# Forgetting sums: a product on TensorE, or loaded across the partitions and added by VectorE

## The chip, the cores and the metric

The kernel runs on one core of a Trainium2 chip. The metric is the device time of one execution in microseconds; lower is better. TensorE multiplies matrices into PSUM, VectorE, ScalarE and GpSimd work element by element, and SyncE issues every DMA of this kernel, in one queue.

## The reference

One decoder block over 512 tokens and 16 meta tokens ahead of them (L = 528). All is f32. One projection of the normed input feeds two attentions of 16 heads each, whose outputs are gated, mixed and normed. The forgetting attention (FoX) adds a sum of log forget gates to its scores:

```python
log_f = jax.nn.log_sigmoid((f_logit + fox_forget_b[l]).astype(jnp.float32)).transpose(0, 2, 1)
cum = jnp.cumsum(log_f, axis=-1)
...
s = jnp.einsum('bhqd,bhkd->bhqk', qb, k, preferred_element_type=jnp.float32) * scale
if cq is not None:
    s = s + (cq[..., :, None] - cum[:, :, None, :])
s = jnp.where(key_pos[None, :] <= qpos[:, None], s, -jnp.inf)
p = jax.nn.softmax(s, axis=-1)
```

The term of the query (`cq`) is the same for a whole row and falls out of the softmax, so only `-cum` of the keys has to reach the scores: one number for each key and head, the same for every query.

## The kernel before

TensorE's instructions stand in the order of the program text; the other engines' are ordered by a scheduler with priorities, and some DMAs are kept in the order of the text. After an opening (norm, small projections, the forget sums) come sixteen attention stages, a forgetting stage and a latent (MLA) stage in turn, each for two heads: `stages = [(br, pr) for pr in range(8) for br in (1, 0)]`, `br` 1 is forgetting. Then the gates and output products follow.

A stage computes scores of all 512 queries of two heads in four query blocks `b` of 128. Block `b` sees 144 + 128 b keys, and only its last 128 need the causal mask. `scores(0)` does blocks 0 to 2 in two PSUM banks a head (0 and 1 together, then 2), `scores(1)` does block 3 in two pieces. Every f32 operand is split into a high and a low half, so a product of two is three products (`hlk`, `hlq` are the split keys and queries). The two heads lie on partitions 0 to 63 and 64 to 127, so a product is a pair of 64-row matmuls, one for each head.

In a forgetting stage there is a fourth pair: the sums `CT` (two rows a head, high and low half of `-cum / SC_FOX`) times `ONE`, which is one on these two rows and zero elsewhere. It spreads the sums over the 128 queries inside the accumulation. `CT` is loaded for each head pair from `c_dram` by two small DMAs, issued from `k_fox`.

Behind the products VectorE reads each piece of scores out of PSUM with one instruction that adds the mask `maskt`, scales by `-scale`, writes `sf` and keeps the smallest value `nb`; a second piece of a block takes the first one's `nb` along. ScalarE takes the exponential in place and sums it up (`su`). `norm` (`n0`, `n1`) scales by `ri`, the reciprocal of `su`, and writes high and low f16 halves `pn` (ScalarE the high, VectorE the low, GpSimd those of the meta keys). DMA transposes bring `pn` into `ptt`, and `values`, which runs in the next stage between its two score parts, multiplies by the values into `ov`; VectorE turns that into `gT`.

Between these parts TensorE works on `fill`: the projections of the gates `z`, and of the next stage's queries, keys and values (`fq`, `fk`, `v`, `mq`, `mk`). They accumulate in three PSUM banks (`accp`), which each take the next result when the one in them has been read: `mq` is read by ScalarE and VectorE into `hlq`, `mk` into `hlk`, `z` into `sil`. Weights come in as `wraw` by DMA and are split into `wh` (ScalarE) and `wl` (GpSimd).

In a forgetting stage the fill is: the gate `z` of the forgetting branch, `mq`, three eighths of the latent branch's `z`, `mk` in two halves, then the rest of that `z` with `v` between.

Of the kernel before, what the change touches and what calls it, by code (L numbers as in the profile page):

```python
# [11 lines left out]
F32 = mybir.dt.float32  # L12
# [5 lines left out]
ALU = mybir.AluOpType  # L18
# [5 lines left out]
S = 512  # L24
META = 16
L = S + META
NH = 16
KD = D // 128
# [10 lines left out]
SC_FOX = 1.0 / math.sqrt(HD)  # L39
NEG = -1.0e30  # L40
# [5 lines left out]
HALF = 272  # L46
# [3 lines left out]
def f32(ap):  # L50
    return ap.bitcast(F32)
# [3 lines left out]
def block_kernel(ctx: ExitStack, tc: tile.TileContext, x, meta_tokens, pre_norm_g, w_in, fox_forget_b,  # L55
                 mla_q_norm_g, mla_kv_norm_g, w_uq, w_ukv, w_br_mla, w_br_fox, w_out, post_norm_g,
                 rope_tok, rope_pe, out):
    nc = tc.nc
# [18 lines left out]
    padp = ctx.enter_context(tc.tile_pool(name="padp", bufs=1, side="right"))  # L77
    pad = padp.tile([128, 56], F32, tag="pad", name="pad")

    c_dram = dram.tile([2, NH, L], F32, tag="cdram", name="c_dram")  # L80
    qpe_dram = dram.tile([NH, 2, 2, 16, S], F32, tag="qpedram", name="qpe_dram")

    wp = ctx.enter_context(tc.tile_pool(name="wp", bufs=3))
    uid = [0]
    written, sums_out = [False], []
    behind, through, first_t, exps, halved, lowered = [], [], [], [], {}, {}

    def dma(out, src, start=None):

        with tc.issue_after(sums_out[1]) if written[0] and len(sums_out) == 2 else nullcontext():  # L90
            ins = (start or nc.sync.dma_start)(out=out, in_=src)
        if written[0]:
            tc.keep_in_program_order(ins)
        return ins.ins

    def mm(*a, **k):
        nc.tensor.matmul(*a, **k)  # L97
# [75 lines left out]
    ths = {}  # L173
# [66 lines left out]
    def hl_done(key, n, w):  # L240

        def done(i, ps):
            if i == 0:
                hls[key] = hlp.tile([128, 2, n], F32R, tag=f"hl{key[0]}", name="hl" + "".join(map(str, key)))
            hl = hls[key]
            o = w * i
            w_ = min(w, n - o)

            with tc.high_priority(offset=30):
                halved[key, i] = nc.scalar.copy(hl[:, 0, o : o + w_], ps).ins  # L250
                lowered[key, i] = split_lo(nc.vector, hl[:, 1, o : o + w_], ps, hl[:, 0, o : o + w_]).ins
        return done
# [2 lines left out]
        return unit(f"fq{pr}", win_w(O_FQ, pr), u_act, KD, REAL, hl_done(("q", 1, pr), S, S))  # L255

    def k_fox(pr):
        halves = hl_done(("k", 1, pr), L, HALF)

        def done(i, ps):  # L260
            halves(i, ps)
            if pr and i:
                for h in range(2):

                    with tc.issue_after(first_t[0]) if pr == 1 else nullcontext():
                        dma(f32(CT[64 * h : 64 * h + 2, :]), c_dram[:, 2 * pr + h, :])
        return unit(f"fk{pr}", win_w(O_FK, pr), u_act, KD, ALLT, done)

# [3 lines left out]
    with ExitStack() as ph:  # L272
# [265 lines left out]
        for i in range(2):  # L538
            for h in range(2):
                nc.sync.dma_start(f32(CT[64 * h + i : 64 * h + i + 1, :]), f32(ch[h : h + 1, i]))  # L540
        for i in range(2):
            sums_out.append(nc.sync.dma_start(c_dram[i], f32(ch[:, i])).ins)

    gctx = ctx.enter_context(ExitStack())
    PAIRED = [i + 4 * j for i in range(4) for j in range(2)]
# [2 lines left out]
    def gate_unit():  # L548

        i, br = gates.pop(0)  # L550

        def done(_, ps):
            ths[i, br] = thp.tile([128, S], F32, tag="th", name=f"th{i}{br}")
            nc.scalar.activation(ths[i, br], ps, AF.Tanh, scale=0.5)
        return unit(f"pg{i}{br}", win_w((O_GA, O_GB)[br], i), u_act, KD, REAL, done)


    with ExitStack() as att:
# [4 lines left out]
        stp = att.enter_context(tc.tile_pool(name="stp", bufs=4, space=PSUM))  # L563
        ovp = att.enter_context(tc.tile_pool(name="ovp", bufs=1, space=PSUM))

        QP = ac.tile([128, S], F32R, tag="QP", name="QP")
        maskt = ac.tile([128, L + 16], BF16, tag="maskt", name="maskt")
        nc.gpsimd.memset(maskt, 0.0)
# [177 lines left out]
        def attention(br, pr):  # L746
# [6 lines left out]
            def sets(h, b, c0, w):  # L753
                hs = slice(64 * h, 64 * h + 64)
                qs, ks = slice(128 * b, 128 * b + 128), slice(c0, c0 + w)
                out = [(q[hs, i, qs], k[hs, j, ks]) for i, j in ((0, 0), (1, 0), (0, 1))]
                if br:
                    return out + [(ONE[hs], CT[hs, ks])]
                return out + [(QP[hs, qs], KP[i][hs, ks]) for i in range(2)]

            sums, sfs = {}, {}
# [2 lines left out]
            def sf_of(h, b):  # L764
                o, n = SF_STEP * (b % 3), 144 + 128 * b
                return sfs[b // 3][:, h, o : o + n]

            def scores(g):

                banks = (((0, 0, 144, 0), (1, 0, 272, 144)), ((2, 0, 400, 0),)) if g == 0 else \  # L770
                    (((3, 0, HALF, 0),), ((3, HALF, L - HALF, 0),))

                def fn():
                    if g == 0:
                        for t in ("nb", "su", "ri"):
                            sums[t] = aw.tile([128, 2, 4], F32, tag=t, name=f"{t}{nm_}")
                    sfs[g] = aw.tile([128, 2, (2 * SF_STEP + 400, L)[g]], F32, tag=f"sf{g}", name=f"sf{nm_}{g}", bufs=1)
                    for ib, parts in enumerate(banks):
                        ps = [stp.tile([128, 512], F32, tag="st", name=f"st{nm_}{g}{ib}{h}") for h in range(2)]
                        for b, c0, w, o in parts:  # L780
                            for i, ops in enumerate(zip(*(sets(h, b, c0, w) for h in range(2)))):
                                for h, (Q, K) in enumerate(ops):
                                    mm(ps[h][:, o : o + w], Q, K, start=(i == 0), stop=(i == 4 - br))
                        for b, c0, w, o in parts:
                            m0 = 384 - 128 * b + c0
                            for h in range(2):
                                nb = sums["nb"][:, h, b : b + 1]

                                with tc.high_priority(offset=100):
                                    nc.vector.tensor_tensor_reduce(  # L790
                                        out=sf_of(h, b)[:, c0 : c0 + w], in0=ps[h][:, o : o + w],
                                        in1=maskt[:, m0 : m0 + w], scale=-scale, scalar=3.0e38 if c0 == 0 else nb,
                                        op0=ALU.add, op1=ALU.min, accum_out=nb)
                    with tc.high_priority(offset=60):
                        for b in GRP[g]:
                            for h in range(2):
                                sf = sf_of(h, b)
                                exps[g] = nc.scalar.activation(sf, sf, AF.Exp, bias=sums["nb"][:, h, b : b + 1],  # L798
                                                               scale=-1.0, accum_out=sums["su"][:, h, b : b + 1]).ins
                return fn  # L800
# [45 lines left out]
                                               op0=ALU.mult, op1=ALU.mult)  # L846

            return scores(0), scores(1), norm(0), norm(1), values

        def in_order():  # L850

# [57 lines left out]
        behind.clear()  # L909
        late = []  # L910
        for si, (br, pr) in enumerate(stages):
            s0, s1, n0, n1, va = attention(br, pr)

            fill = fills[si]
            for fn in [s0] + late:
                fn()
            if si == 0:
                run(fill[:3])
            s1()

            if si == 0:

                run(fill[3:5])
                run(vts[1, 0] + pe_rest)
# [6 lines left out]
                first_t.extend(through)  # L931
                run(fill[5:])
            else:
                if si == 1:

                    written[0] = True
                    for x in range(2):
                        store0(x, 2, 8)
                    written[0] = False
                run(fill[:5])  # L940
                if si == 1:

                    behind[:] = exps[:1]
# [254 lines left out]
```

## Time and profile before

| | us |
|---|---|
| median of three runs | 600.92 (600.5 to 601.12) |
| the profiled execution | 601.22 |
| its span in the profile | 599.2 |
| TensorE busy | 590.7 |
| VectorE, ScalarE, GpSimd busy | 374.3, 342.4, 179.4 |

Some 2 us lie around the span. Rows of the profile read: start or busy time, engine, line of the kernel, operation, the tile written and those read, and the shape. The granted TensorE clock is 0.999 of full speed. The kernel moved 58.10 MB from HBM and 4.00 MB to it.

### The profile page before, as it was taken

The page shows a single profiled execution, that of the slowest core. Times are in us where ns is not written, and L with a number is a line of the kernel's source. Part 1 is how long each engine was busy: PE and PEld are TensorE (multiplying, and loading weights), DVE is VectorE, ACT ScalarE, POOL GpSimd, SP SyncE. Part 2 cuts the span into 40 slices and gives each one's busy share as a digit, 9 for nine tenths or more (in the row PEclk, how much of TensorE's full clock was granted, in tenths as well). Part 3 has the DMA queues.
Part 4 walks back from the last instruction along what each step waited for, and adds up shares of the span by engine and source line. Part 5 has one row for each costly group of instructions (what it writes and reads, how often), then busy time and mean ns, then how long its engine had stood idle before and what let it go on. Part 6 is the DMA issues. An engine that isn't in the chain of part 4 may idle for free.

```text
span 599.2 us, 10724 instructions
## 1 busy us (share of the span) xinstructions
PE 590.7 (99%) x3777; PEld 501.3 (84%) x3777; DVE 374.3 (62%) x1004; ACT 342.4 (57%) x786; POOL 179.4 (30%) x239
## 2 busy tenths in 40 slices
PE   8999999999999999999999999999999999999996
PEld 6989889889889888898898898878888888888884
DVE  5946776774675675766657747764633524367857
ACT  7847775784674675766758747852222423353753
POOL 4316544444348353433524534430000000000000
PEclk9999999999999999999999999999999999999999
DMA  8532889988885998796896878788534333333603
GB/s 288 117 83 88 158 177 250 205 184 181 159 163 124 200 212 203 143 200 139 172 192 136 179 157 176 170 161 291 175 85 106 106 92 84 105 106 93 224 0 141
DMA packets 217910, 93.22 MB, mean 156 GB/s; under 512 B 131372, under 2 KB 209588, under 8 KB 217856
## 3 DMA queue, kind: packets, MB, share of 16 engines
q1 hardware_dynamic: 217856, 92.54, 66.3%
q8 instruction: 29, 0.48, 0.3%
q14 instruction: 25, 0.20, 0.1%
HBM read 58.10 MB, written 4.00 MB: 104 GB/s over the span
## 4 chain that ended last, share of the span: by engine, by line
PE 96%; ACT 2%; DMA 1%; issue 0%; SPq 0%; DVE 0%; POOL 0%; DVEq 0%; ACTq 0%; POOLq 0%
PE z L97 17%; PE pg L97 15%; PE py L97 15%; PE st L97 9%; PE v L97 9%; PE fk L97 8%; PE fq L97 8%; PE ov L97 5%; PE x L97 4%; PE psm L97 3%; PE mq L97 2%; PE mk L97 1%; PE ppe L97 1%; PE y L97 1%; DMA wsr<-in_w_in_dram 1%; ACT uTh L382 0%
## 5 line engine op out<-in xcount | busy, mean ns | idle before, releaser
L103 POOL TENSOR_TENSOR wl<-wraw,wh 128x1024 fp32r<-128x1024 f32 (+2 forms) x62 | 120.1, 1945 | 104.2 <-ACT wh L130 75.6
L130 ACT CAST wh<-wraw 128x1024 fp32r<-128x1024 f32 (+1 forms) x80 | 83.0, 1041 | 115.7 <-PE pg L97 38.5
L798 ACT ACTIVATE sf<-sf,nb 128x144 f32<-128x144 f32 (+3 forms) x128 | 72.0, 564 | 8.3 <-DVE nb L790 8.2
L826 DVE SCALAR_TENSOR_TENSOR pn<-sf,ri,pn 128x128 f16<-128x128 f32 (+3 forms) x128 | 68.7, 575 | 12.4 <-ACT pn L825 12.3
L825 ACT ACTIVATE pn<-sf,ri 128x128 f16<-128x128 f32 (+3 forms) x128 | 61.5, 551 | 19.9 <-ACT sf L798 17.2
L103 DVE TENSOR_TENSOR wl<-wraw,wh 128x1024 fp32r<-128x1024 f32 x34 | 41.6, 1223 | 43.7 <-ACT wh L130 43.5
L790 DVE CUSTOM_DVE_ANT_0 sf<-st,maskt 128x272 f32<-128x272 f32 (+2 forms) x128 | 48.7, 435 | 4.0 <-PE st L97 3.9
L97 PE MATMUL z<-uTh,wh 128*128 128x512 f32 x128 | 50.9, 398 | 0.0
L97 PE MATMUL pg<-uTh,wh 128*128 128x512 f32 x128 | 50.3, 393 | 0.0
L97 PE MATMUL z<-uTl,wh 128*128 128x512 f32 x128 | 50.0, 391 | 0.0
L97 PE MATMUL z<-uTh,wl 128*128 128x512 f32 x128 | 50.0, 390 | 0.0
L97 PE MATMUL pg<-uTl,wh 128*128 128x512 f32 x128 | 49.8, 389 | 0.0
L97 PE MATMUL pg<-uTh,wl 128*128 128x512 f32 x128 | 49.8, 389 | 0.0
L97 PE MATMUL py<-gh,wh 128*128 128x512 f32 x128 | 49.8, 389 | 0.0
L97 PE MATMUL py<-gl,wh 128*128 128x512 f32 x128 | 49.8, 389 | 0.0
L97 PE MATMUL py<-gh,wl 128*128 128x512 f32 x128 | 49.8, 389 | 0.0
L97 PE MATMUL st<-hlk,hlq 64*128 64x272 f32 (+3 forms) x480 | 47.3, 306 | 0.0
L97 PEld LDWEIGHTS st<-hlk,hlq 64*128 64x128 f32 x480 | 35.0, 185 | 5.8 <-ACT vh L722 2.8
L703 DVE TENSOR_REDUCE vsc<-v 128x1 f32<-128x272 f32 (+1 forms) x32 | 13.2, 432 | 37.9 <-PE v L97 37.9
L97 PE MATMUL v<-uTh,wl 128*128 128x256 f32 (+1 forms) x128 | 36.5, 285 | 0.0
L97 PE MATMUL fk<-uTl,wh 128*128 128x256 f32 (+1 forms) x128 | 36.4, 285 | 0.0
L97 PE MATMUL fk<-uTh,wh 128*128 128x256 f32 (+1 forms) x128 | 36.4, 285 | 0.0
(233 smaller groups left out, 1430.1 us busy)
## 6 DMA issues: line engine op xcount, KB each, us to landing
wraw<-in_w_in_dram SPq DMA_DIRECT2D x56, 512.0 KB
wraw<-in_w_br_fox_dram SPq DMA_DIRECT2D x8, 512.0 KB
tb<-in_w_out_dram SPq DMA_DIRECT2D x8, 512.0 KB
wraw<-in_w_br_mla_dram SPq DMA_DIRECT2D x8, 512.0 KB
wraw<-in_w_out_dram SPq DMA_DIRECT2D x6, 512.0 KB
xr<-in_x_dram SPq DMA_DIRECT2D x4, 512.0 KB
out_dram<-yo SPq DMA_DIRECT2D x8, 256.0 KB
QP<-qpe_dram SPq DMA_DIRECT2D x7, 256.0 KB
```

Of the source, the lines that this page charges most:

```text
L97: nc.tensor.matmul(*a, **k)
L103: return eng.tensor_tensor(out=lo, in0=src, in1=f32(hi), op=ALU.subtract)
L130: nc.scalar.copy(wh[:, :n], raw[:, :n])
L703: nc.vector.tensor_reduce(out=sc[:, i : i + 1], in_=ps, op=ALU.max, axis=AX.X, apply_absolute_value=True)
L790: nc.vector.tensor_tensor_reduce(out=sf_of(h, b)[:, c0 : c0 + w], in0=ps[h][:, o : o + w], in1=maskt[:, m0 : m0 + w], scale=-scale, scalar ...
L798: exps[g] = nc.scalar.activation(sf, sf, AF.Exp, bias=sums["nb"][:, h, b : b + 1], scale=-1.0, accum_out=sums["su"][:, h, b : b + 1]).ins
L825: nc.scalar.activation(hi, sf, AF.Copy, scale=rib)
L826: nc.vector.scalar_tensor_tensor(out=lo, in0=sf, scalar=rib, in1=hi, op0=ALU.mult, op1=ALU.subtract)
```

## The change

In the seven forgetting stages of head pairs 1 to 7 the fourth pair of products is gone. The sums of both heads are loaded from `c_dram` once a pair, each spread over 128 partitions by the load itself (`cbp`). GpSimd makes a second copy with the causal mask in it (`cbm`: the meta columns copied, the 512 others through a select). VectorE's reduce adds these f32 tiles in place of the bf16 mask. Since a block's unmasked and masked columns now stand in two tiles, a reduce over both becomes two (`added`). `c_dram` holds one f32 row a head instead of two halves, made by one GpSimd multiply. The two pairs of tiles live in the pool of the gates' results `th`, whose tiles grow from 512 to 528 columns. Pair 0 keeps its product.

```diff
-    c_dram = dram.tile([2, NH, L], F32, tag="cdram", name="c_dram")
+    c_dram = dram.tile([NH, L], F32, tag="cdram", name="c_dram")
...
     def k_fox(pr):
-        halves = hl_done(("k", 1, pr), L, HALF)
-
-        def done(i, ps):
-            halves(i, ps)
-            if pr and i:
-                for h in range(2):
-
-                    with tc.issue_after(first_t[0]) if pr == 1 else nullcontext():
-                        dma(f32(CT[64 * h : 64 * h + 2, :]), c_dram[:, 2 * pr + h, :])
-        return unit(f"fk{pr}", win_w(O_FK, pr), u_act, KD, ALLT, done)
+        return unit(f"fk{pr}", win_w(O_FK, pr), u_act, KD, ALLT, hl_done(("k", 1, pr), L, HALF))
...
-        for i in range(2):
-            sums_out.append(nc.sync.dma_start(c_dram[i], f32(ch[:, i])).ins)
+        nc.gpsimd.tensor_scalar(out=fa[:, 2], in0=fa[:, 0], scalar1=-1.0 / SC_FOX, scalar2=None, op0=ALU.mult)
+        sums_out.append(nc.sync.dma_start(c_dram, fa[:, 2]).ins)
...
+        cb = [[thp.tile([128, L], F32, tag="th", name=f"cb{n}{h}") for h in range(2)] for n in "pm"]
...
                 if br:
-                    return out + [(ONE[hs], CT[hs, ks])]
+                    return out if pr else out + [(ONE[hs], CT[hs, ks])]
...
+            def added(h, b, c0, c1):
+
+                if not (br and pr):
+                    return [(c0, c1, maskt[:, 384 - 128 * b + c0 : 384 - 128 * b + c1])]
+                d = META + 128 * b if b else 0
+                return [(a, e, cb[n][h][:, a:e]) for n, a, e in ((0, c0, min(c1, d)), (1, max(c0, d), c1)) if a < e]
...
                                 nb = sums["nb"][:, h, b : b + 1]
-
-                                with tc.high_priority(offset=100):
-                                    nc.vector.tensor_tensor_reduce(
-                                        out=sf_of(h, b)[:, c0 : c0 + w], in0=ps[h][:, o : o + w],
-                                        in1=maskt[:, m0 : m0 + w], scale=-scale, scalar=3.0e38 if c0 == 0 else nb,
-                                        op0=ALU.add, op1=ALU.min, accum_out=nb)
+                                for a, e, in1 in added(h, b, c0, c0 + w):
+
+                                    with tc.high_priority(offset=100):
+                                        nc.vector.tensor_tensor_reduce(
+                                            out=sf_of(h, b)[:, a:e], in0=ps[h][:, o + a - c0 : o + e - c0],
+                                            in1=in1, scale=-scale, scalar=3.0e38 if a == 0 else nb,
+                                            op0=ALU.add, op1=ALU.min, accum_out=nb)
...
+        def bias(pr):
+
+            for h in range(2):
+                plain, masked = cb[0][h], cb[1][h]
+                nc.sync.dma_start(plain, c_dram[2 * pr + h : 2 * pr + h + 1].broadcast_to([128, L]))
+                nc.gpsimd.tensor_copy(masked[:, 0:META], plain[:, 0:META])
+                nc.gpsimd.affine_select(out=masked[:, META:].rearrange("p (b c) -> p b c", c=128),
+                                        in_=plain[:, META:].rearrange("p (b c) -> p b c", c=128),
+                                        pattern=[[0, 4], [-1, 128]], base=0, channel_multiplier=1,
+                                        compare_op=ALU.is_ge, fill=NEG)
...
                 n0()
+                if not (br or last):
+                    bias(pr + 1)
                 run(fill[5:11])
```

The scheduler places the other engines' instructions anew. VectorE in the forgetting stage of pair 1, from the second bank of `scores(0)` into `scores(1)`; before (`ISA` rows are the reduces, those of `nb` alone read out the minimum):

```order
L790 ISA sf_1443,nb_1440<-st_1466,maskt 128x400
L790 ISA nb_1440 128x1
L790 ISA sf_1443,nb_1440<-st_1467,maskt 128x400
L790 ISA nb_1440 128x1
L806 TENSOR_SCALAR su_1441<-su_1441 128x2x3
L807 RECIPROCAL ri_1442<-su_1441 128x2x3
L845 SCALAR_TENSOR_TENSOR gT_777<-ov_1484,vsc_1094,sil_1121 128x512
L826 SCALAR_TENSOR_TENSOR pn_724<-sf_1443,ri_1442,pn_724 128x128
L790 ISA sf_1512,nb_1440<-st_1513,maskt 128x272
L790 ISA nb_1440 128x1
L790 ISA sf_1512,nb_1440<-st_1514,maskt 128x272
L790 ISA nb_1440 128x1
```

and now:

```order
L791 ISA sf_1455,nb_1452<-st_1476,cbp_718 128x272
L791 ISA nb_1452 128x1
L791 ISA sf_1455,nb_1452<-st_1477,cbm_721,nb_1452 128x128
L791 ISA nb_1452 128x1
L791 ISA sf_1455,nb_1452<-st_1476,cbm_720,nb_1452 128x128
L791 ISA nb_1452 128x1
L846 SCALAR_TENSOR_TENSOR gT_781<-ov_1494,vsc_1098,sil_1125 128x512
L791 ISA sf_1522,nb_1452<-st_1523,cbp_718 128x272
L791 ISA nb_1452 128x1
L791 ISA sf_1522,nb_1452<-st_1524,cbp_719 128x272
L791 ISA nb_1452 128x1
L791 ISA sf_1522,nb_1452<-st_1533,cbp_718,nb_1452 128x128
```

The block of 400 columns is read in 272 and 128, with `nb` as a further operand of the second; `su`, `ri` and the first `pn` no longer stand ahead of the last block.

ScalarE in the same stage, from the exponentials (`sf`) to `hlq`; before:

```order
L798 ACTIVATE sf_1443,su_1441<-sf_1443,nb_1440 128x272
L798 ACTIVATE sf_1443,su_1441<-sf_1443,nb_1440 128x400 x2
L825 ACTIVATE pn_724<-sf_1443,ri_1442 128x128 x2
L825 ACTIVATE pn_724<-sf_1443,ri_1442 128x2x128 x2
L825 ACTIVATE pn_724<-sf_1443,ri_1442 128x3x128 x2
L798 ACTIVATE sf_1512,su_1441<-sf_1512,nb_1440 128x528 x2
L825 ACTIVATE pn_725<-sf_1512,ri_1442 128x4x128 x2
L130 CAST wh_1806<-wraw_1544 128x1024
L738 ACTIVATE sil_1593<-z_1546 128x512
L250 CAST hlq_1611<-mq_1604 128x512
```

and now:

```order
L799 ACTIVATE sf_1455,su_1453<-sf_1455,nb_1452 128x400 x2
L799 ACTIVATE sf_1522,su_1453<-sf_1522,nb_1452 128x528 x2
L826 ACTIVATE pn_728<-sf_1455,ri_1454 128x128 x2
L826 ACTIVATE pn_728<-sf_1455,ri_1454 128x2x128 x2
L826 ACTIVATE pn_728<-sf_1455,ri_1454 128x3x128 x2
L826 ACTIVATE pn_729<-sf_1522,ri_1454 128x4x128
L730 ACTIVATE sil_1601<-z_1554 128x512
L826 ACTIVATE pn_729<-sf_1522,ri_1454 128x4x128
L130 CAST wh_1814<-wraw_1552 128x1024
L250 CAST hlq_1619<-mq_1612 128x512
```

The exponentials of the last block (528 columns) come ahead of all `pn`, and `sil` moves between the last two `pn`; the weight cast still stands ahead of `hlq`.

SyncE's queue behind the same stage's scores; before:

```order
L91 DMA wraw_1619<-in_w_in_dram 128x8x128
L91 DMA CT<-c_dram 2x528
L91 DMA_TRANSPOSE pt<-pn_724 128x6x128
L91 DMA CT<-c_dram 2x528
L91 DMA_TRANSPOSE pt<-pn_724 128x10x128
L91 DMA_TRANSPOSE pt<-pn_724 128x14x128
L91 DMA_TRANSPOSE pt<-pn_725 128x18x128
L91 DMA wraw_1810<-in_w_in_dram 128x8x128
```

and now:

```order
L91 DMA wraw_1627<-in_w_in_dram 128x8x128
L855 DMA cbp_718<-c_dram 128x528
L855 DMA cbp_719<-c_dram 128x528
L91 DMA_TRANSPOSE pt<-pn_728 128x6x128
L91 DMA_TRANSPOSE pt<-pn_728 128x10x128
L91 DMA_TRANSPOSE pt<-pn_728 128x14x128
L91 DMA_TRANSPOSE pt<-pn_729 128x18x128
L91 DMA wraw_1818<-in_w_in_dram 128x8x128
```

The loads of the next pair's sums stand ahead of the stage's four transposes; the loads into `CT` that stood among them are gone.

More of the change, by code (lines that the diff above doesn't have):

```diff
@@ L85, in block_kernel @@
     written, sums_out = [False], []
-    behind, through, first_t, exps, halved, lowered = [], [], [], [], {}, {}
+    behind, through, exps, halved, lowered = [], [], [], {}, {}
     def dma(out, src, start=None):
-        with tc.issue_after(sums_out[1]) if written[0] and len(sums_out) == 2 else nullcontext():
+        with tc.issue_after(sums_out[0]) if written[0] and sums_out else nullcontext():
             ins = (start or nc.sync.dma_start)(out=out, in_=src)
@@ L552, in done @@
         def done(_, ps):
-            ths[i, br] = thp.tile([128, S], F32, tag="th", name=f"th{i}{br}")
+            ths[i, br] = thp.tile([128, L], F32, tag="th", name=f"th{i}{br}")[:, 0:S]
             nc.scalar.activation(ths[i, br], ps, AF.Tanh, scale=0.5)
@@ L766, in sf_of @@
                 return sfs[b // 3][:, h, o : o + n]
+            last_set = (4, 2 if pr else 3)[br]
+            def added(h, b, c0, c1):
[3 more added lines that the diff above has]
+                return [(a, e, cb[n][h][:, a:e]) for n, a, e in ((0, c0, min(c1, d)), (1, max(c0, d), c1)) if a < e]
             def scores(g):
@@ L782, in fn @@
                                 for h, (Q, K) in enumerate(ops):
-                                    mm(ps[h][:, o : o + w], Q, K, start=(i == 0), stop=(i == 4 - br))
+                                    mm(ps[h][:, o : o + w], Q, K, start=(i == 0), stop=(i == last_set))
                         for b, c0, w, o in parts:
-                            m0 = 384 - 128 * b + c0
                             for h in range(2):
                                 nb = sums["nb"][:, h, b : b + 1]
-                                with tc.high_priority(offset=100):
-                                    nc.vector.tensor_tensor_reduce(
-                                        out=sf_of(h, b)[:, c0 : c0 + w], in0=ps[h][:, o : o + w],
-                                        in1=maskt[:, m0 : m0 + w], scale=-scale, scalar=3.0e38 if c0 == 0 else nb,
-                                        op0=ALU.add, op1=ALU.min, accum_out=nb)
+                                for a, e, in1 in added(h, b, c0, c0 + w):
[4 more added lines that the diff above has]
+                                            op0=ALU.add, op1=ALU.min, accum_out=nb)
                     with tc.high_priority(offset=60):
@@ L911, in block_kernel @@
         for si, (br, pr) in enumerate(stages):
+            last = si + 1 == len(stages)
             s0, s1, n0, n1, va = attention(br, pr)
@@ L930, in block_kernel @@
                 n1()
-                first_t.extend(through)
                 run(fill[5:])
```

## The prediction

> **What bounds the kernel now.** I read the page first: its busy line, then the chain that ended last.
>
> ```profile
> PE 590.7 (99%) x3777; PEld 501.3 (84%) x3777; DVE 374.3 (62%) x1004; ACT 342.4 (57%) x786; POOL 179.4 (30%) x239
> PE 96%; ACT 2%; DMA 1%; issue 0%; SPq 0%; DVE 0%; POOL 0%; DVEq 0%; ACTq 0%; POOLq 0%
> ```
>
> TensorE is the bound: 96% of the chain is its own work, no other engine holds over 2%. An instruction taken off TensorE shortens the program by its issue time, unless a result of another engine then comes too late. So two things are wanted: the price of the removed products, and the waits that stand just behind TensorE. The timeline of the second forgetting stage (head pair 1, 103.27 to 122.40 us) shows both. First TensorE (start, duration, instruction; merged rows have a count).
>
> ```profile
> 103.27 0.56 PE L97 MATMUL st<-hlk,hlq 64*128 64x144 f32 x6
> 103.66 0.28 PE L97 MATMUL st<-CT,ONE 64*128 64x144 f32 x2
> 103.77 0.58 PE L97 MATMUL st<-hlk,hlq 64*128 64x272 f32 x6
> 104.19 0.28 PE L97 MATMUL st<-CT,ONE 64*128 64x272 f32 x2
> 104.32 0.72 PE L97 MATMUL st<-hlk,hlq 64*128 64x400 f32 x6
> 104.86 0.36 PE L97 MATMUL st<-CT,ONE 64*128 64x400 f32 x2
> ...
> 107.60 0.29 PE L97 MATMUL st<-CT,ONE 64*128 64x272 f32 x2
> 107.72 0.51 PE L97 MATMUL st<-hlk,hlq 64*128 64x256 f32 x6
> 108.07 0.28 PE L97 MATMUL st<-CT,ONE 64*128 64x256 f32 x2
> ...
> 117.70 0.35 PE L97 MATMUL mk<-cTh,wh 128*128 128x256 f32 x1
> 117.89 0.28 PE L97 MATMUL mk<-cTl,wh 128*128 128x256 f32 x1
> ...
> 122.40 0.56 PE L97 MATMUL st<-hlk,hlq 64*128 64x144 f32 x6
> ```
>
> The durations overlap; what counts is start to next start. A pair of products (one for each head) takes one slot: three 400-wide pairs fill 104.32 to 104.86, 0.18 us each.
>
> The two rows of `mk` show the only place in the stage where TensorE already slips. The second half of the latent keys (`mk`) takes over the accumulator bank that `mq` filled, so it must wait until VectorE has read `mq` into `hlq`. Its first product lasts 0.35 instead of 0.28 us, and the next starts 0.07 us late. VectorE's rows at this place, here and in a later forgetting stage (head pair 6), with TensorE's matching row of that one:
>
> ```profile
> 116.93 0.68 DVE L103 TENSOR_TENSOR hlq<-mq,hlq 128x512 fp32r<-128x512 f32 x1
> ...
> 330.45 0.68 DVE L103 TENSOR_TENSOR hlq<-mq,hlq 128x512 fp32r<-128x512 f32 x1
> ...
> 331.42 0.29 PE L97 MATMUL mk<-cTl,wh 128*128 128x256 f32 x1
> ```
>
> `hlq` ends at 117.61 and the second `mk` product starts at 117.89, 0.28 later; in the other stage it ends at 331.13 and the product starts at 331.42, 0.29 later. The product follows `hlq`, so this is a wait with no room at all: **TensorE gains in a stage only as far as `hlq` also comes earlier.**
>
> **What is removed.** Ten products a stage, five slots: 0.11 (103.66 to 103.77), 0.13 (104.19 to 104.32), 0.18 (the 400-wide price above), 0.12 (107.60 to 107.72), and 0.12 for the 256-wide one (three pairs fill 107.72 to 108.07). That is 0.66 us a stage, 4.6 us in seven stages. With the present slip of 0.07 gone too, the most that can be won is 0.73 a stage, 5.1 us.
>
> **What is added on the path to `hlq`.** VectorE reads the same 1,344 score columns of each head, but in eight pieces instead of five, because the masked and the plain sums stand in two tiles: sixteen reducing instructions instead of ten. The first three blocks are now followed, without a break, by `gT` and the last block, and only then come the sums' reciprocals. ScalarE takes the exponentials of the last block ahead of all `pn`. So I walk the chain anew with the durations of the stage before.
>
> ```profile
> 104.62 0.31 DVE L790 CUSTOM_DVE_ANT_0 sf<-st,maskt 128x144 f32<-128x144 f32 x1 [0.42 <-PE st L97]
> 104.85 0.08 DVE L790 DVE_READ_ACCUMULATOR2_ANT nb<- 128x1 f32 x1
> 104.85 0.44 DVE L790 CUSTOM_DVE_ANT_0 sf<-st,maskt 128x272 f32<-128x272 f32 x1
> ...
> 105.22 0.30 DVE L790 CUSTOM_DVE_ANT_0 sf<-st,maskt 128x144 f32<-128x144 f32 x1
> ...
> 105.80 0.57 DVE L790 CUSTOM_DVE_ANT_0 sf<-st,maskt 128x400 f32<-128x400 f32 x1
> ...
> 106.30 0.57 DVE L790 CUSTOM_DVE_ANT_0 sf<-st,maskt 128x400 f32<-128x400 f32 x1
> ...
> 108.46 0.71 DVE L845 SCALAR_TENSOR_TENSOR gT<-ov,vsc,sil 128x512 f32<-128x512 f32 x1
> 109.09 0.42 DVE L826 SCALAR_TENSOR_TENSOR pn<-sf,ri,pn 128x128 f16<-128x128 f32 x1
> ...
> 110.42 0.47 DVE L790 CUSTOM_DVE_ANT_0 sf<-st,maskt,nb 128x256 f32<-128x256 f32 x1
> ...
> 110.82 0.47 DVE L790 CUSTOM_DVE_ANT_0 sf<-st,maskt,nb 128x256 f32<-128x256 f32 x1
> ```
>
> Again start to start: a 144-wide reduce takes 0.23, a 272-wide one 0.37, a 400-wide one 0.50, so 128 columns are worth 0.13; `gT` takes 0.63. The 256-wide form that carries the minimum of the piece before it (`nb` as a scalar) takes 0.40. No row shows the new 128-wide piece of that form: from the 256-wide row less 128 columns it is 0.27, which I take, since form and operands are the same. Its bounds: 0.21 (the plain 144-wide row less 16 columns, no price for the scalar) and 0.40 (the carried row undiminished). The added operand is f32 in place of bf16; the hlq rows, with two f32 operands, go 512 columns in 0.68, no slower per column, so I add nothing for it.
>
> ScalarE:
>
> ```profile
> 104.97 0.42 ACT L798 ACTIVATE sf<-sf,nb 128x144 f32<-128x144 f32 x1 [0.28 <-DVE nb L790]
> ...
> 108.63 2.51 ACT L825 ACTIVATE pn<-sf,ri 128x128 f16<-128x128 f32 x6 [0.51 <-ACT sf L798]
> 111.04 0.72 ACT L798 ACTIVATE sf<-sf,nb 128x528 f32<-128x528 f32 x1
> ...
> 111.76 0.72 ACT L798 ACTIVATE sf<-sf,nb 128x528 f32<-128x528 f32 x1
> ...
> 113.52 1.34 ACT L825 ACTIVATE pn<-sf,ri 128x512 f16<-128x512 f32 x2 [0.95 <-ACT sf L798]
> 114.76 1.04 ACT L130 CAST wh<-wraw 128x1024 fp32r<-128x1024 f32 x1
> 115.71 0.58 ACT L738 ACTIVATE sil<-z 128x512 f32<-128x512 f32 x1
> 116.19 0.57 ACT L250 CAST hlq<-mq 128x512 fp32r<-128x512 f32 x1
> ```
>
> An exponential starts 0.04 after its minimum was read out (104.93 to 104.97). Steps: 0.72 for a 528-wide exponential, 2.41 for six `pn`, 0.62 for one 512-wide `pn`, 0.95 for the weight cast, 0.48 for `sil`, 0.57 for `hlq`.
>
> The walk: VectorE's first reduce starts 0.24 earlier, by the two slots gone ahead of it, at 104.38. First bank, four 144-wide (0.92) and two carried pieces (0.54): 105.84. Second bank, two 272-wide (0.74) and two carried: 107.12. `gT`: 107.75. Last block, two 272-wide: 108.49; three carried pieces: 109.30, readout and hand-over 0.12: 109.42. ScalarE: two exponentials 110.86, six `pn` 113.27, `pn`, `sil`, `pn` 114.99, cast 115.94, `hlq` 116.51. VectorE's `hlq`: 0.04 + 0.68, 117.23. TensorE's second `mk` product, 0.28 on: **117.51 instead of 117.89, 0.38 earlier.** Without that wait it would stand at 117.89 - 0.73 = 117.16, so TensorE waits 0.35 there, about half of what the products gave. Seven stages: 2.7 us.
>
> A shorter wait lies ahead of it: VectorE lets the second score bank go at about 107.2, just when TensorE wants it (107.72 less four slots, 107.18). 0.1 or 0.2 lost there comes out of the 0.35, not on top.
>
> [...]
>
> **What is added off the path.** Per head pair two loads of 128 x 528 f32, and on GpSimd two 16-wide copies and two 512-wide selects. Against the wait they could bring stand these rows (GpSimd, SyncE's queue, TensorE):
>
> ```profile
> 44.12 0.30 POOL L569 TENSOR_SCALAR_AFFINE_SELECT maskt<-maskt 128x128 bf16<-128x128 bf16 x1
> ...
> 57.60 1.28 POOL L663 TENSOR_TENSOR pt<-pt 128x512 f32<-128x512 f32 x1
> ...
> 112.35 6.56 SPq L91 DMA_TRANSPOSE pt<-pn  x3
> 119.00 0.54 SPq L91 DMA_DIRECT2D wraw<-in_w_in_dram  x1
> ...
> 124.70 0.63 PE L97 MATMUL ov<-pt,vp 80*64 80x512 f16 x4
> ```
>
> A select costs between 0.30 (a quarter of the columns) and 1.28 (two operands); I take 0.8, so 2 us a pair on an engine that is busy 30%, in the latent stage, after the forgetting stage has ended. Behind it wait the meta columns' `pn` and weight halves that TensorE has not reached. Nothing on the path. The loads stand ahead of the forgetting stage's four transposes in SyncE's queue, and wait until VectorE has last read the plain tile, 109.0; the first `pn` is ready only after ScalarE's 110.86. The transposes are issued until 118.91 and first used at 124.70: 5.8 us of cover, of which 2.2 (108.63 to 110.86) and 1.1 for issuing two loads (0.54 each, the weight load's row) are used up. The fourteen small loads into `CT` go. The single GpSimd multiply and one store in place of two, in the opening, stand behind the first heads' loads: nothing.
>
> **Rivals.** (a) The whole gain: the carried piece costs 0.21 to 0.22, seven of them stand on the path (2 + 2 + 3), and the 0.35 vanish: 5.1 us, 595.8. For it: that the accumulator's readout hides in the rows as it is. Against: the 256-wide row, which pays 0.14 over its columns (0.40 less 0.26).
> (b) No change: all sixteen reduces pay the carried row's fixed 0.14, not 0.08 to 0.09 as the plain rows do. That alone takes about 0.4 of VectorE's time on the path, and the 0.38 is gone: 601. Against: rows that went back to back just as these will. [...]
> (c) Slower: VectorE's second reduce of a block waits for the first one's minimum to land. Then a carried piece takes 0.40, as long as the 256-wide row: 7 x 0.13 = 0.91 later at `hlq`, 0.53 lost a stage, 3.7 us, 604.6. It turns from gain to loss at 0.27 + 0.38/7 = 0.32. Against: one reduce of the other head stands between a minimum and its use. The same sign would follow if the transposes came 2 us later still; nothing suggests it.
> That the products stay is ruled out: the built program's TensorE order has lost exactly 70 of them and is otherwise the same.
>
> **How the numbers follow.** The walk is made on the profiled execution, 601.22 us by its own time; the median is 600.92. The sum is taken off the median: 600.92 - 2.7 = 598.2. Chances: forecast 0.50, (a) 0.22, (b) 0.14, (c) 0.14. A change within 0.2%, 1.2 us, cannot be told from none here. (a) and the forecast are faster, 0.72; (b) same, 0.14; (c) slower, 0.14. The range takes in (a) at the low end and (b) at the high end, 595.8 to 601.4.
>
> **What would show it.** Right: forgetting stages of pairs 1 to 7 last 18.7 to 18.8 us instead of 19.13; carried pieces step 0.27; `hlq` ends near 13.96 us after the stage's first product (before 14.34), and the second `mk` product 0.28 behind it. Wrong: stages of 18.4 (then (a)); carried steps of 0.32 and up; a wait of TensorE at `st`, `ov` or a weight instead of `mk`; latent stages longer than before.

## Result and the profile after

| | us, median of 12 runs | range | profiled execution, its span |
|---|---|---|---|
| before | 600.84 | 600.39 to 601.91 | 601.22, 599.2 |
| after | 599.48 | 599.05 to 600.26 | 599.89, 598.0 |

The ratio is 0.9976, 95% interval 0.9968 to 0.9985: 1.4 us faster, where 2.7 was forecast. The sign was right and the time lies in the range; the gain is half as large.

The page after, busy line and chain:

```profile
PE 588.3 (98%) x3707; PEld 498.0 (83%) x3707; DVE 385.5 (64%) x1088; ACT 343.6 (57%) x786; POOL 199.4 (33%) x268
PE 65%; DVE 1%; issue 0%; DVEq 0%; ACT 0%
```

The chain goes back no further than 198 us, to VectorE in pair 3's forgetting stage, so its shares sum to 66%. TensorE has lost its 70 products and 2.4 us of busy time, and it now waits inside the attention part. These are the two rows that are new in its list of waits (total, times, longest):

```profile
PE ov L97 <- issue: 1.1, 1, 1.1
PE mk L97 <- DVE hlq L103: 0.2, 1, 0.2
```

The same forgetting stages before and after, in the view by windows (window; its length and busy PE, PEld, DVE, ACT, POOL, with instructions; then granted clock, DMA share, GB/s). Before, pairs 1 to 3:

```profile
103.27:122.40 19.13, 19.13 (x133) 15.53 (x132) 13.12 (x45) 14.13 (x35) 7.71 (x11) 1.00 0.92 209
145.43:164.57 19.14, 19.14 (x133) 15.54 (x133) 13.14 (x45) 14.13 (x35) 7.71 (x11) 1.00 0.87 167
190.40:209.52 19.12, 19.12 (x134) 15.54 (x134) 13.06 (x45) 14.14 (x35) 9.87 (x15) 1.00 0.86 165
```

After, pairs 1, 2, 3 and 7:

```profile
102.72:122.47 19.75, 18.64 (x124) 15.10 (x124) 14.81 (x57) 14.30 (x35) 10.70 (x15) 1.00 1.03 231
145.50:164.31 18.81, 18.81 (x124) 15.04 (x124) 14.19 (x57) 14.29 (x35) 9.62 (x15) 1.00 0.94 172
190.14:209.21 19.07, 18.88 (x123) 15.05 (x122) 15.01 (x57) 14.29 (x35) 12.21 (x19) 1.00 0.84 185
...
357.90:376.71 18.81, 18.81 (x124) 15.04 (x124) 14.18 (x57) 14.30 (x35) 8.13 (x11) 1.00 0.78 161
```

The stages of pairs 2 and 7 are as forecast within 0.1 us. Pair 1's is longer than before: TensorE is busy 18.64 of 19.75 us, the rest is the wait at `ov`. Pair 3's won almost nothing.

Pair 2's stage in the timeline after, TensorE, VectorE and ScalarE at the places of the walk:

```profile
148.91 1.18 PE L97 MATMUL st<-hlk,hlq 64*128 64x272 f32 x12
...
159.33 0.29 PE L97 MATMUL mk<-cTh,wl 128*128 128x272 f32 x1
159.59 0.38 PE L97 MATMUL mk<-cTh,wh 128*128 128x256 f32 x1
159.81 0.28 PE L97 MATMUL mk<-cTl,wh 128*128 128x256 f32 x1
```

```profile
146.62 0.31 DVE L791 CUSTOM_DVE_ANT_0 sf<-st,cbm 128x144 f32<-128x144 f32 x1 [0.18 <-PE st L97]
...
149.34 0.74 DVE L846 SCALAR_TENSOR_TENSOR gT<-ov,vsc,sil 128x512 f32<-128x512 f32 x1
150.01 0.43 DVE L791 CUSTOM_DVE_ANT_0 sf<-st,cbp 128x272 f32<-128x272 f32 x1
...
151.26 0.35 DVE L791 CUSTOM_DVE_ANT_0 sf<-st,cbm,nb 128x128 f32<-128x128 f32 x1
...
151.54 0.34 DVE L791 CUSTOM_DVE_ANT_0 sf<-st,cbm,nb 128x128 f32<-128x128 f32 x1
...
158.84 0.69 DVE L103 TENSOR_TENSOR hlq<-mq,hlq 128x512 fp32r<-128x512 f32 x1 [0.50 <-ACT hlq L250]
```

```profile
151.74 0.74 ACT L799 ACTIVATE sf<-sf,nb 128x528 f32<-128x528 f32 x1 [1.21 <-DVE nb L791]
...
157.29 1.04 ACT L130 CAST wh<-wraw 128x1024 fp32r<-128x1024 f32 x1
158.23 0.58 ACT L250 CAST hlq<-mq 128x512 fp32r<-128x512 f32 x1
```

A carried 128-wide piece steps 0.28 here (151.26 to 151.54) and 0.27 elsewhere; `hlq` ends at 159.53, 14.03 after the stage's start at 145.50, and the second `mk` product starts 0.28 behind it.

### The profile page after: what moved, and what is told of

Same layout as the page of the kernel before. It is cut to its first block, busy times and chain, and to the rows that moved or that the text cites. A ratio compares the mean times of both kernels' runs of the same rounds, so it can differ in the third digit from the quotient of the medians.

```text
span 598.0 us, 10750 instructions
## 1 busy us (share of the span) xinstructions
PE 588.3 (98%) x3707; PEld 498.0 (83%) x3707; DVE 385.5 (64%) x1088; ACT 343.6 (57%) x786; POOL 199.4 (33%) x268
## 4 chain that ended last, share of the span: by engine, by line
PE 65%; DVE 1%; issue 0%; DVEq 0%; ACT 0%
PE py L97 15%; PE pg L97 14%; PE z L97 10%; PE st L97 5%; PE v L97 5%; PE fk L97 4%; PE fq L97 4%; PE x L97 4%; PE ov L97 3%; PE mq L97 1%; PE y L97 1%; DVE pn L827 1%; PE mk L97 1%; DVE yo L1120 0%; DVEq L1208 0%
## 5 line engine op out<-in xcount | busy, mean ns | idle before, releaser
L103 POOL TENSOR_TENSOR wl<-wraw,wh 128x1024 fp32r<-128x1024 f32 (+2 forms) x62 | 121.6, 1969 | 90.0 <-ACT wh L130 59.2
L799 ACT ACTIVATE sf<-sf,nb 128x272 f32<-128x272 f32 (+3 forms) x128 | 72.5, 567 | 17.6 <-DVE nb L791 16.3
L827 DVE SCALAR_TENSOR_TENSOR pn<-sf,ri,pn 128x128 f16<-128x128 f32 (+3 forms) x128 | 72.4, 605 | 6.9 <-ACT pn L826 5.7
L97 PE MATMUL st<-hlk,hlq 64*128 64x272 f32 (+3 forms) x480 | 45.8, 308 | 0.0
L97 PE MATMUL v<-uTl,wh 128*128 128x256 f32 (+1 forms) x128 | 36.4, 285 | 0.0
```

The lines of the kernel that those rows point to most:

```text
L103: return eng.tensor_tensor(out=lo, in0=src, in1=f32(hi), op=ALU.subtract)
L827: nc.vector.scalar_tensor_tensor(out=lo, in0=sf, scalar=rib, in1=hi, op0=ALU.mult, op1=ALU.subtract)
```

## Experiments

Stage lengths below are the distances between the first `st` products of neighbouring stages in a kernel's profiled execution. Times are medians, beside the kernel before on the same chip. "Sum" is the change of the seven stages together against before (133.88 us).

| kernel | pair 1 | 2 | 3 | 4 | 5 | 6 | 7 | sum | median, its before | ratio, 95% |
|---|---|---|---|---|---|---|---|---|---|---|
| before | 19.14 | 19.14 | 19.12 | 19.13 | 19.14 | 19.08 | 19.13 | | | |
| after | 19.74 | 18.81 | 19.08 | 18.86 | 18.87 | 18.83 | 18.81 | -0.9 | 599.48, 600.84 | 0.9976 (0.9968 to 0.9985) |
| after again | 18.84 | 18.84 | 19.06 | 18.84 | 18.84 | 18.84 | 18.83 | -1.8 | 600.01, 600.80 | 0.9984 (0.9975 to 0.9993) |
| products out only | 23.99 | 18.40 | 18.40 | 18.40 | 18.40 | 18.40 | 18.40 | +0.5 | 601.25, 600.80 | 1.0003 (0.9994 to 1.0012) |
| pieces only | 19.13 | 19.13 | 19.13 | 19.14 | 19.14 | 19.12 | 19.13 | 0.0 | 600.85, 600.87 | 1.0001 (0.9992 to 1.0010) |
| cast behind `hlq` | 18.85 | 18.62 | 18.62 | 19.01 | 18.75 | 18.98 | 18.64 | -2.4 | 599.30, 600.80 | 0.9973 (0.9964 to 0.9982) |
| before, cast behind | 19.07 | 19.07 | 19.07 | 19.07 | 19.07 | 19.07 | 19.07 | -0.4 | 600.62, 601.00 | 0.9992 (0.9984 to 1.0001) |
| late loads | 23.62 | 18.81 | 18.86 | 18.84 | 18.85 | 18.85 | 18.84 | +2.8 | 605.00, 600.80 | 1.0066 (1.0054 to 1.0079) |
| pair 1 without loads | 18.84 | 18.82 | 19.07 | 18.84 | 18.84 | 18.80 | 18.80 | -1.9 | 599.88, 601.00 | 0.9983 (0.9974 to 0.9992) |
| early, late | 19.57 | 18.84 | 18.83 | 18.84 | 18.84 | 18.84 | 18.84 | -1.3 | 600.06, 601.00 | 0.9985 (0.9976 to 0.9994) |
| early, late, cast | 19.68 | 18.62 | 18.64 | 18.62 | 18.62 | 18.64 | 18.62 | -2.4 | 599.12, 601.00 | 0.9965 (0.9953 to 0.9978) |
| ScalarE queue, 59 us | 19.46 | 18.59 | 18.64 | 18.62 | 18.62 | 18.64 | 18.62 | -2.7 | 598.44, 601.00 | 0.9954 (0.9940 to 0.9967) |
| ScalarE queue, 65 us | 18.62 | 18.62 | 18.64 | 18.62 | 18.62 | 18.64 | 18.62 | -3.5 | 598.04, 600.87 | 0.9952 (0.9939 to 0.9964) |

**The changed kernel again**, unedited.

> The changed kernel once more, for a second trace of it. Theory A (the loss in pair 1's stage belongs to the change: the loads of the sums push the transposes back in SyncE's queue): TensorE waits again about 1 us at `ov` in pair 1's forgetting stage, which lasts 19.5 to 19.8. Theory B (an accident of that one execution): no wait at `ov`, the stage lasts 18.8 to 18.9, like those of pairs 2 and 4 to 7. Both: the other forgetting stages 18.8 to 19.1, the time 1 to 2 us under the kernel before.

Pair 1's stage is 18.84 here and TensorE does not wait at `ov`: the loss of 0.9 in the first trace is not in every execution. Pair 3's 19.06 came back.

**Products out, nothing in.** The kernel before with this edit, and the flag that closes an accumulation moved to the third product:

```diff
-                    return out + [(ONE[hs], CT[hs, ks])]
+                    return out if pr else out + [(ONE[hs], CT[hs, ks])]
```

> The kernel before with the five slots of products of the forget sums left out in each of pairs 1 to 7 and nothing put in their place (the sums are not added to the scores there). This is what the removal alone can bring. If the half is lost to the pieces added on VectorE: stages 18.4, about 4.6 to 5 us less than before. If the chain through ScalarE to `hlq` would eat it in any case: stages 18.6 to 18.8, 2.5 to 3.5 us less than before. What lies between this and the changed kernel is what loads, selects and pieces cost together.

Six stages last 18.40, exactly 0.73 less than before, so the removal is worth what the slots said, and the chain through ScalarE does not stop it. TensorE in pair 2's stage (start 150.84; compare 148.91, 159.59 and 159.81 above):

```profile
154.26 0.99 PE L97 MATMUL st<-hlk,hlq 64*128 64x272 f32 x12
...
164.49 0.29 PE L97 MATMUL mk<-cTh,wl 128*128 128x272 f32 x1
164.61 0.28 PE L97 MATMUL mk<-cTh,wh 128*128 128x256 f32 x1
164.73 0.28 PE L97 MATMUL mk<-cTl,wh 128*128 128x256 f32 x1
```

The last block's products take 0.99 here and 1.18 in the changed kernel: 0.19 is a wait for the second score bank. The first two `mk` products start 0.12 apart instead of 0.22, and the first of them follows its forerunner after 0.12 instead of 0.26: 0.24 is the wait for `hlq`. Together 0.43, and 0.73 - 0.43 = 0.30 is what undisturbed stages won. Pair 7's stage of the changed kernel, in which no select for a next pair runs, is 18.81 too, so what it loses against 18.40 belongs to the pieces. The time of this kernel says nothing on the gain: its scheduler put more `CT` loads ahead of the first latent stage's transposes, and pair 1's stage lost 5.6 us (below).

**Pieces in, products kept.** The kernel before with its reduces cut as in the changed one:

```diff
+                            d = META + 128 * b if br and pr and b else c0
...
+                                for a, e in ((c0, min(c0 + w, d)), (max(c0, d), c0 + w)):
```

> The kernel before with its products, its loads and its mask, only the reduces of pairs 1 to 7 cut into the sixteen pieces of the changed kernel. If the pieces cost what the walk gives them (0.27 for a carried one) and the products leave TensorE behind VectorE, `hlq` ends at 14.04 + 0.24 = 14.28 and stages stay at 19.06 to 19.13, time within 0.5 us of before. If the pieces cost more than that beside an unchanged TensorE, stages of 19.3 and up, 1 us or more slower.

No change. VectorE's pieces cost only what TensorE would otherwise gain.

**The cast behind `hlq`.** In the changed kernel ScalarE casts the next query weight (0.95 us) just ahead of `hlq`; here it comes after.

```diff
+                if not br and si > 1:
+                    behind[:] = [halved[("q", 0, pr), 0]]
                 run(fill[:5])
+                if not br and si > 1:
+                    behind.clear()
```

> The changed kernel with one thing moved: on ScalarE the cast of the next query weight (0.95 us) goes behind the cast of `hlq` in each forgetting stage of pairs 1 to 7. If what eats half of the gain is the chain ScalarE, `hlq` on ScalarE, `hlq` on VectorE, second `mk` product, then the wait at `mk` is gone and the stages come down from 18.8 toward 18.4, up to 0.35 x 7 = 2.4 us less than the changed kernel. If it is the rate at which VectorE takes the scores or its `pn`, the stages stay at 18.8, within 0.3 us of the changed kernel.

Three stages come to 18.62 to 18.64: the wait at `mk` is gone, the 0.19 at the score bank stays. The others stop at 18.75 to 19.01, which the selects explain (experiment "Late loads").

> The kernel before with the cast moved behind that of `hlq`, as a control: does the cast's place matter without the change? There TensorE slips only 0.07 a stage at `mk`, so at most 0.5 us less, stages 19.06 to 19.13. If the cast's place were worth as much here as in the changed kernel (0.2 a stage), stages of 18.9 and 1.4 us less.

The control: the same edit in the kernel before gives 0.07 a stage, just its slip at `mk`.

**Late loads.** The loads of the next pair go behind the latent stage's own transposes, and with them GpSimd's copies and selects. TensorE, VectorE and ScalarE keep their order.

```diff
+                with tc.issue_after(through[0]):
+                    nc.sync.dma_start(plain, c_dram[2 * pr + h : ...
```

> The changed kernel with the loads of the next pair's sums queued on SyncE behind the latent stage's own `pt` transposes, so that loads and GpSimd's copies and selects fall in the latent stage; TensorE, VectorE and ScalarE keep their order. If the two losses (1.1 us at `ov` in pair 1, and VectorE's `pn` drawn out from 0.75 to 1.03-1.18 beside the selects in pairs 3 to 6) come from there: all seven stages 18.75 to 18.85, `pn` at 0.75, 1 to 1.5 us less than the changed kernel, as forecast 598.2. If they do not: pair 1's stage stays at 19.7, time within 0.3 us of the changed kernel. A delay of the latent stage's last transposes behind the loads would show as a wait at `ov` in the forgetting stage's start.

Half right. Pair 3's stage comes from 19.08 to 18.86. The changed kernel there, GpSimd and VectorE:

```profile
200.93 0.64 POOL L857 TENSOR_SCALAR_AFFINE_SELECT cbm<-cbp 128x512 f32<-128x512 f32 x1
201.52 0.66 POOL L816 CAST pn<-mt 128x32 f16<-128x32 f32 x1
...
202.49 0.19 POOL L856 COPY cbm<-cbp 128x16 f32<-128x16 f32 x1
202.63 0.64 POOL L857 TENSOR_SCALAR_AFFINE_SELECT cbm<-cbp 128x512 f32<-128x512 f32 x1
```

```profile
202.63 1.18 DVE L827 SCALAR_TENSOR_TENSOR pn<-sf,ri,pn 128x512 f16<-128x512 f32 x1
203.73 0.68 DVE L103 TENSOR_TENSOR hlq<-mq,hlq 128x512 fp32r<-128x512 f32 x1
```

And with late loads:

```profile
206.28 0.75 DVE L827 SCALAR_TENSOR_TENSOR pn<-sf,ri,pn 128x512 f16<-128x512 f32 x1
207.52 0.69 DVE L103 TENSOR_TENSOR hlq<-mq,hlq 128x512 fp32r<-128x512 f32 x1 [0.50 <-ACT hlq L250]
```

A select that runs while VectorE does the last low half of `pn` draws that from 0.75 out to 1.18; the select before it draws the seven smaller ones out to 3.76 in all, against 3.37 in pair 2's stage. In the seven stages of the changed kernel's trace the last one takes 0.75 with an overlap of at most 0.14, 0.85 with 0.31, 1.03 with 0.48 to 0.49 and 1.18 with 0.64, so it is the selects and not the loads: the copy at 202.49 already reads what the last load brought, ahead of `pn`. `hlq` then starts as soon as `pn` ends, no longer half a microsecond after it for ScalarE: VectorE is late, not ScalarE. GpSimd's small cast, 0.30 in the late-load kernel's stage, takes 0.66 here. In the other stages the same stretching is covered, until the cast is moved: then it shows as 18.75 to 19.01.

But pair 1's stage is 4.5 us longer than before, and all timed runs are slower (603.7 to 606.3). There the late loads fall into the first latent stage, issued from 96.66, still ahead of its last transpose, and from 103.15, behind the start of pair 1's stage at 102.86. VectorE then waits for the select on the second load:

```profile
107.81 0.31 DVE L791 CUSTOM_DVE_ANT_0 sf<-st,cbm 128x144 f32<-128x144 f32 x1 [3.29 <-POOL cbm L858]
```

TensorE waits for the transposes and for VectorE:

```profile
105.25 2.04 PE L97 MATMUL ov<-pt,vp 80*64 80x512 f16 x26 [0.87 <-DMA pt<-pn]
108.77 0.88 PE L97 MATMUL st<-hlk,hlq 64*128 64x272 f32 x6 [1.49 <-DVE nb L791]
110.04 0.79 PE L97 MATMUL st<-hlk,hlq 64*128 64x256 f32 x6 [0.39 <-DVE nb L791]
```

TensorE's idle time here is 2.75 us, and its first `z` comes 7.90 after the stage's start instead of 4.53 in the second trace of the changed kernel, 3.4 later. The rest is TensorE's clock, which was granted 0.90, 0.50 and 0.75 in the three 2 us windows from 110 to 116 (0.2 + 1.0 + 0.5 us lost). Less the 0.24 at `mk`, which falls away, that is the 4.8 over 18.84. The kernel without products shows the same after a wait of 3.85 at `ov`:

```profile
106.00:108.00 2.00, 0.00 (x0) 0.00 (x0) 1.20 (x6) 1.13 (x2) 0.00 (x1) 1.00 1.26 295
108.00:110.00 2.00, 0.80 (x6) 0.54 (x8) 0.00 (x0) 2.00 (x9) 2.00 (x1) 0.91 0.21 47
110.00:112.00 2.00, 2.00 (x16) 1.52 (x14) 0.00 (x0) 0.95 (x4) 0.35 (x1) 0.50 0.69 164
112.00:114.00 2.00, 2.00 (x23) 1.70 (x20) 1.18 (x4) 0.00 (x0) 0.00 (x0) 0.74 1.09 307
```

The 1.1 us wait of the changed kernel left the clock at 1.00 in each 2 us window from 104 to 116.

**Where pair 1's stage stands.** Its `ov` products need the transposes of the first latent stage. The last of them in SyncE's queue, before and after:

```profile
98.00 4.01 SPq L91 DMA_TRANSPOSE pt<-pn  x1
```

```profile
99.67 3.55 SPq L91 DMA_TRANSPOSE pt<-pn  x1
```

Before, it is issued by 102.01, 1.26 ahead of the stage's start; after, by 103.22, 0.50 behind it, and TensorE waits. In the second trace of the changed kernel it is 102.53, 0.66 ahead, and there is no wait.

The row of the wait names no releaser (`issue`), but the traces agree: no wait at `ov` where the last transpose is issued 0.66 or more ahead, 0.2 at 0.31 ahead, 0.9 to 1.2 at 0.24 to 0.55 behind, 3.9 at 3.06 behind. Where `ov` waits it starts 2.0 to 2.3 after that issue has ended. It wanted to start 1.88 after the stage's start before, and 1.45 now that three slots ahead of it are gone. So the room was about 1.0 us before (1.88 + 1.26 - 2.1), and the change itself takes 0.43 of it; the second trace stands at the edge.

Pair 1's own loads (0.54 MB, issued at 73.1 in the second trace) lie in front; its stages start within 0.1 us of those before, and SyncE's queue is 0.4 to 1.5 us behind at each later entry up to there. Four experiments take these loads away or move them.

Without them (two writes of zero on GpSimd; pair 1's sums left out):

> The changed kernel with pair 1's two loads replaced by two writes of zero on GpSimd (pair 1's forget sums are left out; copies, selects and all pieces stay). If these 0.54 MB, moved while the DMA engines are full, are what brings the transposes of the first latent stage to or past the edge: last transpose issued by 102 us as before, no wait at `ov`, pair 1's stage 18.84, and the median 0.5 to 1 us under the changed kernel. If the transposes are late for another reason (VectorE and ScalarE giving `pn` at another time), pair 1's stage varies on between 18.8 and 19.7 and the median stays.

In the trace as expected: issued by 101.94, 1.33 ahead, 18.84. The median is not lower than the changed kernel's, though 0.5 to 1 us less was expected. So what pair 1 costs on average in the timed runs is not settled; the trace and the timed run can differ there.

Issued at the head of the attention part (`spread(1)`), those of the other pairs late:

```diff
+        spread(1)
         for si, (br, pr) in enumerate(stages):
...
+            if pr > 1:
+                with tc.issue_after(through[0]):
+                    spread(pr)
```

> The changed kernel with pair 1's loads issued at the head of the attention part, ahead of stage 0's transposes, and those of pairs 2 to 7 behind the latent stage's own transposes; the orders of TensorE, VectorE and ScalarE are kept. If the timed loss against the forecast lies in pair 1's stage, where the loads push the transposes to the edge of their use, the wait at `ov` does not come back in any run: all seven stages 18.81 to 18.86, 7 x 0.29 = 2.0 us less than before, about 598.8, and the runs lie closer together. If the loads are not it, the median stays at 599.5 to 600.

> The kernel with early and late loads, and in addition the cast of the next query weight behind that of `hlq`. If two waits share the loss, 0.24 at `mk` for `hlq` and 0.19 at the second score bank for VectorE's pieces, this takes the first away in every stage and leaves the second: all seven stages 18.62 to 18.64, 7 x 0.51 = 3.6 us less than before, about 597.2. If VectorE's `pn` beside GpSimd's selects was not what made three stages 18.75 to 19.01 when the cast alone was moved, they stay there and the gain is about 2.7 us.

The first was wrong: pair 1's stage takes 19.57 with 1.0 at `ov`. Behind the loads the transpose of the values (`vp`) takes 4.7 instead of 1.7, the eight `QP` loads after it (a part of the latent queries) come late, and the last transpose is issued by 103.53 instead of 102.01. In the second, the other six stages are 18.62 to 18.64 as expected, with pair 1's at 19.68 and 0.6 lost already one stage earlier, at the `ov` of the first latent stage. Pairs 4 to 6, at 18.75 to 19.01 with the cast alone, were thus held up by the loads and selects in that place. Late loads move both; the stretched `pn` says that it was the selects.

From ScalarE's queue, first at 59 us, then at 65 us, where the DMA engines have little to do (a share of 0.25 from 65 to 70 us in the second trace). Both kernels have the other pairs' loads late and the cast behind `hlq` as well. The edit of the second:

```diff
+                (nc.scalar if pr == 1 else nc.sync).dma_start(cb[0][h], c_dram[2 * pr + h : ...
...
             if si == 0:
+                with tc.issue_after(exps[0]):
+                    spread(1)
                 run(fill[:3])
```

> The kernel with late loads for pairs 2 to 7 and the cast behind `hlq`, and pair 1's loads issued from ScalarE's queue after its `vh` casts (about 60 us, before a stretch in which the DMA engines are a quarter busy), so that nothing is put into SyncE's queue ahead of stage 0. If queue order and the full DMA engines made pair 1's loss: all seven stages 18.62 to 18.64, 597.2, and no run above 598. If moving the bytes anywhere in the first 100 us suffices for the loss: pair 1's stage 19.3 to 19.7 and 598.2.

> As the kernel with pair 1's loads on ScalarE's queue, but issued there after the six exponentials of stage 0's first three blocks (about 65 us instead of 59), so that they do not stand beside the transposes of `vp` at 60 us, which took 4.4 us there instead of 1.7. If pair 1's wait at `ov` comes from bytes put ahead of SyncE's queue at 60 us: `QP` is issued from 62.4 again, no wait at `ov`, all seven stages 18.62 to 18.64, about 597.8. If the bytes cost the same wherever they go: pair 1's stage 19.3 to 19.7 again, about 598.4.

At 59 us the `vp` transpose beside them takes 4.4 us instead of 1.7 and pair 1's stage 19.46; at 65 us all seven stages are clean:

```profile
103.55:122.17 18.62, 18.62 (x125) 15.00 (x124) 14.01 (x57) 14.27 (x35) 8.14 (x11) 1.00 0.86 184
145.19:163.81 18.62, 18.62 (x123) 15.00 (x122) 14.02 (x57) 14.26 (x35) 8.13 (x11) 1.00 0.82 145
```

This kernel has the lowest median, 598.04, 0.9952 of before; the timings alone do not tell it from the one at 59 us (0.9954), the traces do. Its sum is -3.5; 0.4 of it is given back in stage 0, which lasts 20.49 instead of 20.09.

## Why the prediction was half right

**What is removed: right.** 0.66 and 0.07 a stage were counted from the slots; without anything put in place, six stages are shorter by 0.73.

**The path to `hlq`: right, its size nearly.** Forecast 0.38 a stage, measured 0.30 to 0.33 where nothing else disturbs. First reduce 1.12 after the start (forecast 1.11), third carried piece of the last block ended 6.04 (6.03), the piece's 0.27 was right. The mis-sized term is "readout and hand-over 0.12": the exponential starts at 151.74, 0.20 after the piece gave way at 151.54. The 0.07 that `hlq` then ends late (14.03 against 13.96) is that. The f32 operand costs nothing, as assumed: the plain pieces of 144 and 272 columns step 0.23 and 0.36 with it, and in the same trace the latent stage's reduces with the bf16 mask step 0.23 and 0.36 too (from 124.06). The wait at the second score bank, put at 0.1 to 0.2 and "out of the 0.35, not on top", is 0.19, with 0.24 left at `mk`.

The two medians, 599.48 and 600.01, lie above the 598.2: the stages won what the walk said within 0.1, and the rest was lost off the path.

**What is added off the path: wrong, twice.** This step failed, and it carries the rest of the miss. First, "in the latent stage, after the forgetting stage has ended": the program asks for the selects there, but they wait for nothing that stands there, only for the loads, and these only for VectorE's last read. So they run in the forgetting stage, beside `pn`, and cost 0.22 in pair 3's stage. The select itself takes 0.63 to 1.06, 0.64 in the median, within the bounds. Second, the cover of 5.8 us was worked out for a load in pair 1's forgetting stage, and for pairs 2 to 7 it holds. Pair 1's loads lie elsewhere, in stage 0, and there I priced nothing, though the transposes behind have only about 1.0 us to spare, and 0.6 once `ov` comes 0.43 earlier. The wrong sign named there, "a wait of TensorE at `st`, `ov`" came true there: between 0 and 0.9 us in two executions.

The sum: seven stages at 0.30 are 2.1; less 0.2 for pair 3 and 0 to 0.9 for pair 1 leaves 1.0 to 1.9. The two traces have 0.9 and 1.8, the two timings 1.4 (0.9 to 1.9) and 0.8 (0.4 to 1.5). The timed kernel without pair 1's loads was not faster, so pair 1's share of the timed miss stays open.

**Rivals.** None came true. The whole gain (a) needed carried pieces of 0.21; only the kernel without any pieces has it. (b) needed plain pieces of 0.29 and 0.42, with 0.14 over their columns; they step 0.23 and 0.36. (c) needed a carried piece of 0.32. That a wait eats half was right: 0.43 of 0.73, of which 0.24 is `hlq`'s. That part can be had back: with the cast behind `hlq` a stage is 0.2 shorter.

## What to carry to other kernels

When an engine is relieved, price the wait that stands behind it, from its last producer backwards; that part of the forecast held within 0.1 us a stage. Then follow every instruction that is added off the path to the wait that really releases it: where the program text asks for it is not where a scheduler puts it. And look at the first pass of a loop apart from the others: its loads have other neighbours, here a queue of transposes with about 1.0 us to spare.

## What was not expected of the hardware

- Two long waits of TensorE were more than lost time: after 3.85 us at once in the kernel without products, and after 2.75 in three pieces within 6 us in the one with late loads, its clock was granted 0.90 to 0.91, 0.50 and 0.74 to 0.75 in three 2 us windows, which cost 1.7 us more; after the changed kernel's 1.1 us it stayed at 1.00.
- VectorE's 512-wide `pn` takes 0.75 alone and 1.18 beside a GpSimd select (0.64 of overlap).
- The same two loads of 0.54 MB, issued between 58 and 73 us, cost pair 1's stage at 103 us between nothing and 1.1 us, by the place; issued from 96.7 and 103.2 they cost 4.8.
